# Moving the operand tiles of a two-layer hybrid decoder kernel to other SBUF addresses with small spacer tiles

## The chip, the cores and the metric

One Trainium2 chip, one core of it. The metric is the device time of one execution in microseconds (us); smaller is better.

## What is computed

Two layers (DEPTH = 2) of a decoder trunk on a residual stream of 256 tokens by 2048 channels, all float32. In each layer the stream is normalised and modulated to `u`, and one wide projection `u @ w_in` feeds three token mixers. Cut to what matters here:

```python
u = rms_norm(x, norm_w) * (1.0 + scale) + shift          # scale, shift, gate from silu(c) @ w_ada
proj = u @ w_in                                           # w_in: 2048 x 19,064
y_fox = fox_attention(fq, fk, fv, log_f) * silu(fg)
y_dsa = dsa_attention(dq, dk, dv, iq, ik, iw) * silu(dg)  # keys chosen by an indexer
y_ssd = rms_norm(ssd_scan(conv(sxbc), dt, a, b, c) * silu(sz))
merged = (sigmoid(mg0) * (y_fox @ w_o_fox) + sigmoid(mg1) * (y_dsa @ w_o_dsa)
          + sigmoid(mg2) * (y_ssd @ w_o_ssd))
return x + gate * (merged @ w_out)
```

## The kernel before

All weights stream once from HBM as half-pieces of 128 partitions x 1024 float32 (512 KB, line L162, tile `raw`, 7 buffers). A half-piece is split into a high part `wh` (ScalarE, L175, 4 buffers) and a low part `wl` (VectorE, L176, 3 buffers); the activations are kept as high and low parts too: `uh`, `ul` for the normalised input, `yh`, `yl` (two tiles each) for the gated attention outputs, `ysh`, `ysl` for the state-space output, `mh`, `ml` for the merged stream. A product is three matmuls on float32r operands: high x high, low x high, high x low.

There are two forms. In `feat` (L213 to L215) the **weights are stationary**: 128 columns of a half-piece are loaded into TensorE and 256 tokens of an activation tile move past them. In `three` (L180 to L182, called by `tok_half` and `tok_group`) the **activations are stationary**: 128 tokens of `uh` or `ul` are loaded, and 512 columns of the half-piece move.

```python
for k in range(nk):                                   # feat
    c = slice(k % 8 * P, k % 8 * P + P)
    mm(ps, lhsT=h[:, c], rhs=ah[:, k, :], ...)        # L213
    mm(ps, lhsT=h[:, c], rhs=al[:, k, :], ...)        # L214
    mm(ps, lhsT=l[:, c], rhs=ah[:, k, :], ...)        # L215
```

A layer goes through these stages. First the token-major projections of the queries, keys and values (`tok_half`; in layer 0 they run in `start` while the modulation from `w_ada` is still being summed on VectorE, L229). Then `feat` products for the gates and the convolution input, with the attention and state-space mixers' small products placed between them by a tick counter. Then the gated merge in three branches (`br` 0, 1, 2): for each of 16 column tiles a `feat` over `uh`, `ul` with 16 k-tiles (48 matmuls) and one over the branch's own tile (`yh`, `yl` with 8 k-tiles, 24 matmuls; `ysh`, `ysl` in branch 2 with 16 k-tiles, 48 matmuls). Last the output projection, `feat` over `mh`, `ml`, 16 times 48 matmuls. During layer 0's second half the modulation of layer 1 is streamed too, some half-pieces of `w_ada` for every weight half-piece. TensorE issues in the order written by hand; the weight stream's work on ScalarE, VectorE and the SP queue is emitted ahead of everything else, in its own order.

SBUF tiles come from pools that are laid out one behind the other from the low end (`const`, `wp` with `raw`, `wh`, `wl`, then `up` with `uh`, `ul`, then `small`, then the pools on the side "left") and from the high end (side "right", with `ysp` for `ysh`, `ysl`). A tile's address thus follows from what was allocated ahead of it. The buffers of `wh` and `wl` are 4096 bytes each per partition and all of them lie at one address modulo 1024; a k-tile of 256 tokens is 1024 bytes, a weight block of 128 columns 512 bytes.

Of the kernel before, what the change touches and what calls it, by code (L numbers as in the profile page):

```python
# [10 lines left out]
F32 = mybir.dt.float32  # L11
# [5 lines left out]
PSUM = bass.MemoryType.PSUM  # L17
DRAM = bass.MemoryType.DRAM

DM, SEQ, DEPTH, P = 2048, 256, 2, 128  # L20
# [35 lines left out]
# modulation: (layer, blocks, first tick, ticks a tile)  # L56
ADA = ((0, range(8, 12), 212, 1.8), (1, range(8), 270, 1.9), (1, range(8, 12), 600, 4.0))
# start: steps by which the modulation runs ahead of its use, loads of x after which a tile of it is loaded
AHEAD, EARLY = 1, (1,)
# ticks between dependent products of a mixer, by layer  # L60
# [9 lines left out]
class Net:  # L70
    def __init__(self, ctx, tc, xT, c, pos, inv, par, w_ada, w_tm, w_ts, w_sm, w_od, outT):
        self.tc, self.nc = tc, tc.nc
        self.xT, self.c, self.pos, self.inv, self.par = xT, c, pos, inv, par
        self.w_ada, self.w_tm, self.w_ts, self.w_sm, self.w_od, self.outT = w_ada, w_tm, w_ts, w_sm, w_od, outT
        pool = lambda **k: ctx.enter_context(tc.tile_pool(**k))
        self.const = pool(name="const", bufs=1)
        self.wp = pool(name="wp", bufs=1)
        self.up = pool(name="up", bufs=1)
        self.small = pool(name="small", bufs=1)
        self.mm = pool(name="mm", bufs=4, space=PSUM)  # L80
        self.mx = pool(name="mx", bufs=4, space=PSUM)
        self.dram = pool(name="dram", bufs=1, space=DRAM)
        self.ada_queue = []
        self.front = -1000000
        self.nticks = 0
        self.lanes = [[], [], []]
        # TensorE issues in emission order: ticks place the mixers' products between the projections'
        ctx.enter_context(tc.manual_schedule(engines={mybir.EngineType.PE}))

# [21 lines left out]
    def spawn(self, n, gen, *after):  # L111
        """queue a mixer's steps; it starts when the jobs it follows have been emitted"""
        job = Layer()
        job.gen, job.after, job.done = gen, after, False
        self.lanes[n].append(job)
        return job
# [17 lines left out]
    @contextmanager  # L134
    def first(self):
        """what the weights' stream needs goes before everything else, in its own order"""
        tc = self.tc
        outer, tc.cur_priority = tc.cur_priority, self.front
        yield
        self.front, tc.cur_priority = tc.cur_priority, outer  # L140
# [4 lines left out]
    def rsqrt(self, out, ss, scale, eps, tag):  # L145
        """out = (ss * scale + eps) ** -0.5"""
        nc = self.nc
        shape = list(ss.shape)
        x, y, t = [self.st(shape, tag + n) for n in ("_x", "_y", "_t")]
        i = t.bitcast(I32)  # L150
        nc.vector.tensor_scalar(x, ss, scale, eps, op0=OP.mult, op1=OP.add)
        nc.vector.tensor_scalar(i, x.bitcast(I32), 1, None, op0=OP.logical_shift_right)
        nc.vector.tensor_scalar(y.bitcast(I32), i, -1, 0x5F3759DF, op0=OP.mult, op1=OP.add)
        for n in range(3):
            nc.vector.tensor_mul(t, y, y)
            nc.vector.scalar_tensor_tensor(t, t, -0.5, x, op0=OP.mult, op1=OP.mult)
            nc.vector.scalar_tensor_tensor(out if n == 2 else y, t, 1.5, y, op0=OP.add, op1=OP.mult)

# [6 lines left out]
    def half(self, src):  # L165
        """half a piece, as high and low parts"""
        with self.first():
            r = self.raw(src)
            h = self.wp.tile([P, 1024], F32R, tag="wh", name="wh", bufs=NWH)
            l = self.wp.tile([P, 1024], F32R, tag="wl", name="wl", bufs=NWL)  # L170
            self.split(h, l, r)
        return h, l
# [11 lines left out]
    def tok_half(self, out, src, k, k0, k1):  # L184
        """two k tiles x 512 columns, activations stationary"""
        h, l = self.half(src)
        for i in range(2):
            c = slice(i * 512, i * 512 + 512)
            for th in range(2):
                s = slice(th * P, th * P + P)  # L190
                self.three(out[th], self.uh[:, k + i, s], self.ul[:, k + i, s], h[:, c], l[:, c], k + i == k0, k + i == k1)

    def tok_group(self, blocks):
        """out[b][th] is a bank [token, 512 columns]"""
        out = [[self.mmbank() for _ in range(2)] for _ in blocks]
        for k in range(0, KT, 2):
            for b, blk in enumerate(blocks):
                src = self.w_tm[self.l, blk, k // 2]
                self.tok_half(out[b], src, k, 0, KT - 1)
                self.tick()  # L200
        return out

    def feat(self, src, ah=None, al=None, nk=KT):
        """weights stationary: a bank half [128 columns, 256 tokens]"""
# [16 lines left out]
    def ada_raw(self, l, blk, n, r=None):  # L221
        """modulation: half of the sum for the feature tile blk * 4 + n // 2; after every second tile the pair is put together"""
# [35 lines left out]
    def load(self, x, ssq, *tmp):  # L258
        """what the first products wait for: silu of c on all partitions, x and its sum of squares"""
# [97 lines left out]
    def rstd_row(self, ssq):  # L357
        """1 / rms of each token, along the free axis of every partition"""
# [15 lines left out]
    def u_tile(self, l, k, t):  # L374
        """u = x * A * rstd + shift, as high and low parts"""
        nc = self.nc
        b = self.mods[l].mod[:, k:k + 1]
        nc.scalar.activation(self.uh[:, k, :], t, AF.Identity, bias=b)  # L378
        nc.vector.scalar_tensor_tensor(self.ul[:, k, :], t, b, self.uh.bitcast(F32)[:, k, :], op0=OP.add, op1=OP.subtract)
# [9 lines left out]
    def start(self, blocks, x, ssq, row, raws, got):  # L389
        """first layer: the modulation arrives by pairs of feature tiles; the first products over each four tiles  # L390
        run as soon as their part of u is there, and add up in SBUF (those of the first two blocks in PSUM)"""
# [64 lines left out]
    def head_rstd(self, t, nh, pool):  # L456
        """1 / rms of each head of t [token, 2, nh * 128]"""
# [11 lines left out]
    def to_heads(self, dst, h0, t, c0, scale=None):  # L469
        """two 128-column blocks of token-major t -> dst[:, h0:h0+2, tokens]"""  # L470
# [11 lines left out]
    def rope(self, v, half, c0, pool):  # L482
        """v [token, 2, heads, dims]: rotate the first 2 * half dims"""
# [32 lines left out]
    def g_small(self, ps, sm, dtt, par, lay, D, pool):  # L516
        """softplus of sdt, log sigmoid of ff, their cumulative sums"""
# [33 lines left out]
        # forget gate: cumulative sums, token-major and as rows (those of the keys)  # L551
# [7 lines left out]
        # state-space decays: cumulative sums by chunk, token-major and as rows  # L559
# [18 lines left out]
    def g_heads(self, n, logits, vals, dst, pool):  # L578
        """causal attention, a head a tick: logits, then softmax and its transpose, then the product with the values"""
# [73 lines left out]
    def g_index(self, iqT, ikT, sm, acc, pool):  # L653
        """scores of the indexer; acc becomes 0 at the selected causal keys and BIG elsewhere"""
# [50 lines left out]
    def gate_y(self, name, y, pool):  # L705
        """y *= 2 * silu(gate); y came with a factor of a half"""
# [10 lines left out]
    def layer(self, l):  # L717
# [3 lines left out]
        # right: y of the attentions, temporaries of both; left: one mixer's operands  # L721
# [27 lines left out]
        if l == 0:  # L749
            # x lies where the transposed heads come later  # L750
# [3 lines left out]
        def got(name, j=0, t=None):  # L754
            """a block of projections is there, token-major: the next steps of its mixer"""
# [5 lines left out]
            elif name == "iq":  # L761
                # indexer queries, transposed, lie where the attention's output comes later
# [47 lines left out]
        for g in range(4):  # L810
# [10 lines left out]
            if g == 0:  # L821
                ysp, close_ys = self.pool("ysp", "right")
                S.ysh = ysp.tile([P, KT, SEQ], F32R, name="ysh")
                S.ysl = ysp.tile([P, KT, SEQ], F32R, name="ysl")
            self.spawn(2, self.g_norm(l, g, S.gate, S.y, sp, S), S.job)
# [6 lines left out]
        gp, close_g = self.pool("gp", "left")  # L832
        hp, close_h = self.pool("hp", "left")
        yhl = []
# [7 lines left out]
        for br in range(3):  # L842
            if br == 2:
                close_h()
                mp, close_m = self.pool("mp", "left")
                mh = mp.tile([P, KT, SEQ], F32R, name="mh")
# [54 lines left out]
    def conv(self, f, dst, sp):  # L901
        """causal depthwise convolution over 128 channels, then SiLU"""
# [112 lines left out]
    def g_norm(self, l, g, gates, y, sp, S):  # L1015
        """gate and group norm, transposed"""
# [42 lines left out]
def _ada_raws(w):  # L1059
    """w [2048, 6144] by feature tile and half of k, transposed"""  # L1060
# [3 lines left out]
def _pack(i):  # L1064
# [12 lines left out]
    # halves [128, 1024] of pieces: two k tiles x 512 columns, or eight k tiles x 128 columns  # L1077
# [29 lines left out]
```

## Time and profile before

| | |
|---|---|
| median of 3 runs | 2466.78 us (2463.59 to 2470.31) |
| profiled execution, span from the first to the last instruction | 2465.1 us |
| TensorE busy | 2418.5 us, 98% of the span, 17256 matmuls |
| VectorE busy | 1752.3 us, 71% |
| ScalarE busy | 1195.9 us, 49% |
| mean HBM traffic | 214 GB/s |
| mean granted TensorE clock | 0.997 of full speed |

The profiled execution's own time is its span, 2465.1 us; the median of the runs shown lies 1.7 us above it. A matmul's busy time runs from its start to its modelled end, and consecutive matmuls overlap: durations of 283 ns stand beside starts that are some 120 ns apart. So what a matmul costs is read from the spacing of the starts, which is the length of a stretch over the number of matmuls in it (a count of a window holds about two that began before it).

### The profile page before, as it was taken

How to read it: one execution, taken by the hardware profiler on the slowest of the kernel's cores; microseconds unless marked ns; L12 is line 12 of the kernel's file. 1: busy time of each engine (PE TensorE's matmuls, PEld its weight loads, DVE VectorE, ACT ScalarE, POOL GpSimd, SP SyncE). 2: the span in 40 equal slices, each digit the busy share in tenths (PEclk: the TensorE clock that was granted, in tenths of full speed). 3: DMA queues.
4: the chain of work that ended last, by engine and by line, in shares of the span. 5: the costliest groups of instructions: out<-in, count | busy, mean ns of one | idle time of the engine just before them, and what ended most of it. 6: DMA issues, size and time to landing. Idle time of an engine off the chain costs nothing.

```text
span 2465.1 us, 43733 instructions
## 1 busy us (share of the span) xinstructions
PE 2418.5 (98%) x17256; PEld 2247.5 (91%) x17256; DVE 1752.3 (71%) x3109; ACT 1195.9 (49%) x1932; POOL 1.8 (0%) x11
## 2 busy tenths in 40 slices
PE   6999999999999999999989999999999999999999
PEld 4778799998899999999978877999999999999999
DVE  8899978777766777776775567767776655666554
ACT  4535656555544444343344655555555444444443
POOL 0000000000000000000000000000000000000000
PEclk9999999999999999999999999999999999999999
DMA  9998434544468888788865544544544667776564
GB/s 341 331 328 290 146 120 138 161 157 159 157 214 281 289 281 288 271 276 269 306 205 184 188 138 146 177 152 153 161 155 162 227 229 238 231 233 229 187 214 155
DMA packets 145216, 527.79 MB, mean 214 GB/s; under 512 B 16369, under 2 KB 16881, under 8 KB 145009
## 3 DMA queue, kind: packets, MB, share of 16 engines
q1 hardware_dynamic: 145010, 525.00, 63.4%
q8 instruction: 135, 2.21, 0.4%
q14 instruction: 71, 0.58, 0.1%
HBM read 520.74 MB, written 4.19 MB: 213 GB/s over the span
## 4 chain that ended last, share of the span: by engine, by line
PE 89%; DVE 5%; DMA 4%; issue 1%; ACT 0%; SPq 0%; DVEq 0%
PE pm L213 19%; PE pm L215 19%; PE pm L214 19%; PE pm L180 8%; PE pm L182 8%; PE pm L181 8%; DMA raw<-w_ada 3%; DVE wl L176 2%; DVE raw L229 2%; PE px L987 1%; PE px L475 1%; PE px L609 1%; PE px L996 1%; DMA raw<-w_od 1%; PE held L181 0%
## 5 line engine op out<-in xcount | busy, mean ns | idle before, releaser
L175 ACT CAST wh<-raw 128x1024 fp32r<-128x1024 f32 x788 | 825.4, 1050 | 1002.0 <-PE pm L214 547.5
L176 DVE TENSOR_TENSOR wl<-raw,wh 128x1024 fp32r<-128x1024 f32 x788 | 959.9, 1222 | 344.1 <-PE pm L215 152.9
L213 PE MATMUL pm<-uh,wh 128*128 128x256 f32 x2848 | 816.5, 287 | 0.0
L215 PE MATMUL pm<-uh,wl 128*128 128x256 f32 x2848 | 805.7, 283 | 1.1 <-DVE wl L176 1.1
L214 PE MATMUL pm<-ul,wh 128*128 128x256 f32 x2848 | 805.0, 283 | 0.0
L213 PEld LDWEIGHTS pm<-uh,wh 128*128 128x128 f32 x2848 | 545.1, 191 | 5.2 <-issue 3.9
L214 PEld LDWEIGHTS pm<-ul,wh 128*128 128x128 f32 x2848 | 545.3, 191 | 2.1 <-issue 1.9
L215 PEld LDWEIGHTS pm<-uh,wl 128*128 128x128 f32 x2848 | 545.1, 191 | 1.6 <-DVE wl L176 1.5
L180 PE MATMUL pm<-wh,uh 128*128 128x512 f32 x896 | 361.1, 403 | 1.1 <-ACT uh L378 1.1
L182 PE MATMUL pm<-wl,uh 128*128 128x512 f32 x896 | 352.1, 393 | 6.9 <-DVE wl L176 6.8
L229 DVE SCALAR_TENSOR_TENSOR raw<-raw,crep 128x1024 f32<-128x1024 f32 x192 | 234.0, 1223 | 174.8 <-DMA raw<-w_ada 174.8
L181 PE MATMUL pm<-wh,ul 128*128 128x512 f32 x896 | 350.7, 391 | 0.0
L182 PEld LDWEIGHTS pm<-wl,uh 128*128 128x128 f32 x896 | 169.0, 189 | 46.2 <-DVE wl L176 10.2
L180 PEld LDWEIGHTS pm<-wh,uh 128*128 128x128 f32 x896 | 169.1, 189 | 39.9 <-issue 3.0
L181 PEld LDWEIGHTS pm<-wh,ul 128*128 128x128 f32 x896 | 169.3, 189 | 35.3 <-issue 1.9
L215 PE MATMUL pm<-mh,wl 128*128 128x256 f32 x512 | 142.5, 278 | 5.2 <-DVE wl L176 4.9
L215 PE MATMUL pm<-ysh,wl 128*128 128x256 f32 x512 | 144.7, 283 | 1.2 <-DVE wl L176 1.2
L214 PE MATMUL pm<-ysl,wh 128*128 128x256 f32 x512 | 144.2, 282 | 0.0
L213 PE MATMUL pm<-ysh,wh 128*128 128x256 f32 x512 | 144.1, 281 | 0.0
L214 PE MATMUL pm<-ml,wh 128*128 128x256 f32 x512 | 141.6, 277 | 1.4 <-DVE ml L176 1.4
L213 PE MATMUL pm<-yh,wh 128*128 128x256 f32 x512 | 142.0, 277 | 0.0
L214 PE MATMUL pm<-yl,wh 128*128 128x256 f32 x512 | 141.8, 277 | 0.0
(315 smaller groups left out, 2814.9 us busy)
## 6 DMA issues: line engine op xcount, KB each, us to landing
raw<-w_ts SPq DMA_DIRECT2D x352, 512.0 KB, 3.9
raw<-w_tm SPq DMA_DIRECT2D x240, 512.0 KB, 3.6
raw<-w_ada SPq DMA_DIRECT2D x192, 512.0 KB, 4.6
raw<-w_od SPq DMA_DIRECT2D x192, 512.0 KB, 4.5
raw<-w_sm SPq DMA_DIRECT2D x4, 512.0 KB, 4.7
xr<-xT SPq DMA_DIRECT2D x4, 512.0 KB, 7.0
x<-xn SPq DMA_DIRECT2D x4, 512.0 KB, 6.4
xr<-x SPq DMA_DIRECT2D x4, 512.0 KB, 6.1
```

What stands on the lines that cost most here:

```text
L175: self.nc.scalar.copy(h, src)
L176: self.nc.vector.tensor_sub(l, src, h.bitcast(F32))
L180: mm(ps, lhsT=ah, rhs=bh, start=start, stop=False)
L181: mm(ps, lhsT=al, rhs=bh, start=False, stop=False)
L182: mm(ps, lhsT=ah, rhs=bl, start=False, stop=stop)
L213: mm(ps, lhsT=h[:, c], rhs=ah[:, k, :], start=k == 0, stop=False)
L214: mm(ps, lhsT=h[:, c], rhs=al[:, k, :], start=False, stop=False)
L215: mm(ps, lhsT=l[:, c], rhs=ah[:, k, :], start=False, stop=k == nk - 1)
L229: nc.vector.scalar_tensor_tensor(r, r, 0.5, self.crep[:, n % 2 * 1024:n % 2 * 1024 + 1024], op0=OP.mult, op1=OP.mult, accum_out=m.part[:, ...
L475: nc.tensor.transpose(ps[:, j * SEQ + th * P:j * SEQ + th * P + P], t[:, th, c0 + j * P:c0 + j * P + P], self.ident)
L609: nc.tensor.matmul(po[:, :SEQ], lhsT=v[:, 0], rhs=pT[:, :SEQ], start=True, stop=False)
L987: nc.tensor.matmul(pd[:, c * 256 + o % 256:c * 256 + o % 256 + 64], lhsT=dec[:, i, c, :], rhs=xd[:, c, o:o + 64], start=True, stop=True)
```

## The change

Five calls of a new helper `pad` put an unused tile into a pool, cleared once by GpSimd so that it exists. Nothing is computed from it; its only effect is on the addresses of the tiles behind it (of `ysh`, `ysl` ahead of it, since that pool grows from the high end). Three of the calls stand in `layer` and run once per layer, so that there are eight clears in all. The rest of the full diff removes comments, and so shifts line numbers by a few.

```diff
         self.const = pool(name="const", bufs=1)
+        self.pad(self.const, 32)
         self.wp = pool(name="wp", bufs=1)
         self.up = pool(name="up", bufs=1)
+        self.pad(self.up, 192)
...
+    def pad(self, pool, nbytes):
+
+        t = pool.tile([P, nbytes // 4], F32, name="pad")
+        self.nc.gpsimd.memset(t, 0.0)
+
...
                 S.ysl = ysp.tile([P, KT, SEQ], F32R, name="ysl")
+                self.pad(ysp, 928)
...
         hp, close_h = self.pool("hp", "left")
+        self.pad(hp, 832)
...
                 mp, close_m = self.pool("mp", "left")
+                self.pad(mp, 832)
```

The start addresses of the tiles in the two built programs, in bytes of a partition modulo 1024, and the distance from the weights to the moving operand:

| tile | before | after | distance before | distance after |
|---|---|---|---|---|
| `wh`, `wl` (and `raw`) | 736 | 768 | | |
| `uh`, `ul` in `feat` | 736 | 960 | 0 | 192 |
| `yh`, `yl` | 928 | 960 | 192 | 192 |
| `ysh`, `ysl` | 864 | 960 | 128 | 192 |
| `mh`, `ml` | 928 | 960 | 192 | 192 |
| `wh`, `wl` moving past `uh`, `ul` (`three`) | 736 | 768 | 0 | -192 |

Without the modulo, the tiles began before at byte 65248 (`wh`), 81632 (`wl`), 93920 (`uh`, which with `ul` ends at 126688), 137120 (`yh`, `mh`) and 174944 (`ysh`). A distance is that of the tiles' starts; the weight blocks and token halves inside the tiles step by 512 bytes, so each distance comes with itself plus 512.

The instructions of TensorE, ScalarE and the SP queue stand in the same order in both programs, and on VectorE one pair of set-up instructions is swapped. GpSimd has the new clears. Its queue in the changed program, from the identity matrix on (`logf` is the clear for the log-forget sums of a layer, the rows `pad 128x232` and `pad 128x208 x2` are those of `ysp` and of `hp` and `mp`):

```order
6 masks.py:197 MEMSET ident 128x128
7 L128 MEMSET pad 128x8
8 L128 MEMSET pad 128x48
9 L551 MEMSET logf 128x80
10 masks.py:199 ISA
11 masks.py:199 AFFINE_SELECT ident<-ident 128x128
12 L306 AFFINE_SELECT tri<-tri 128x128
13 L311 AFFINE_SELECT msk<-msk 128x128 x2
14 L128 MEMSET pad 128x232
15 L128 MEMSET pad 128x208 x2
16 L551 MEMSET logf 128x80
17 L128 MEMSET pad 128x232
```

Before, rows 7, 8, 14, 15 and 17 are not there (nor a last one like row 15, which follows row 17), and nothing else differs in this queue.

## Rows read from the trace of the kernel before

**Rows 1.** The page: the engines' busy time, and the chain that ended last

```profile
PE 2418.5 (98%) x17256; PEld 2247.5 (91%) x17256; DVE 1752.3 (71%) x3109; ACT 1195.9 (49%) x1932; POOL 1.8 (0%) x11
...
PE 89%; DVE 5%; DMA 4%; issue 1%; ACT 0%; SPq 0%; DVEq 0%
```

**Rows 2.** Busy time by stretch: start, layer 0's merge and output projection, layer 1's merge

```profile
core 0: us, PE busy (x) PEld busy (x) DVE busy (x) ACT busy (x) POOL busy (x), PEclk, DMA share, GB/s
0.00:230.00 230.00, 201.83 (x832) 160.06 (x833) 207.09 (x360) 103.13 (x145) 1.61 (x10) 0.99 0.92 332
700.00:1026.00 326.00, 326.00 (x2761) 325.78 (x2760) 233.01 (x333) 139.32 (x162) 0.00 (x0) 1.00 0.82 277
1026.00:1250.00 224.00, 215.12 (x1799) 211.76 (x1798) 162.91 (x257) 88.83 (x112) 0.00 (x0) 1.00 0.84 284
1905.00:2180.00 275.00, 275.00 (x2335) 275.00 (x2334) 170.74 (x218) 119.20 (x138) 0.00 (x0) 1.00 0.70 230
```

**Rows 3.** Matmuls by moving or stationary tile: duration ns min/median/max (views of uh, yh, ysh, mh)

```profile
L213 PE MATMUL pm<-uh,wh x2848: 277/283/682, 230.0 to 2368.7; 128*128 128x256 f32 x190
L213 PE MATMUL pm<-yh,wh x512: 276/276/286, 705.1 to 2191.2; 128*128 128x256 f32 x171
L213 PE MATMUL pm<-ysh,wh x512: 274/281/287, 976.8 to 2374.4; 128*128 128x256 f32 x171
L213 PE MATMUL pm<-mh,wh x512: 276/276/337, 1158.4 to 2461.5; 128*128 128x256 f32 x171
L180 PE MATMUL pm<-wh,uh x896: 387/389/803, 39.2 to 1867.0; 128*128 128x512 f32 x180
```

**Rows 4.** Stretches of one kind alone: uh/ul moving, mh/ml moving, weights moving past uh/ul

```profile
1882.00:1904.00 22.00, 22.00 (x185) 22.00 (x185) 16.19 (x34) 9.81 (x16) 0.00 (x0) 1.00 0.51 169
2400.00:2460.00 60.00, 60.00 (x532) 60.00 (x531) 29.70 (x32) 20.49 (x20) 0.00 (x0) 1.00 0.53 173
1322.00:1342.00 20.00, 20.00 (x90) 16.56 (x89) 15.12 (x49) 7.88 (x9) 0.00 (x0) 1.00 0.59 196
```

**Rows 5.** The chain in layer 0's merge, branch 0: start us, us, what

```profile
705.21 0.12 PE pm L213
713.69 0.12 PE pm L213
722.17 0.12 PE pm L213
```

**Rows 6.** The timeline in layer 1's merge: a matmul and the next one's weight load

```profile
2150.22 0.28 PE L213 MATMUL pm<-uh,wh 128*128 128x256 f32 x1
2150.22 0.19 PEld L214 LDWEIGHTS pm<-ul,wh 128*128 128x128 f32 x1
2150.34 0.28 PE L214 MATMUL pm<-ul,wh 128*128 128x256 f32 x1
```

**Rows 7.** Costliest groups of the two forms: busy us, mean ns

```profile
L214 PE MATMUL pm<-ul,wh 128*128 128x256 f32 x2848 | 805.0, 283 | 0.0
L214 PE MATMUL pm<-ysl,wh 128*128 128x256 f32 x512 | 144.2, 282 | 0.0
```

**Rows 8.** Waits from 700 to 1026: who waited for whom, us in total, times, longest

```profile
ACT wh L175 <- PE pm L214: 120.4, 67, 1.9
DVE raw L229 <- DMA raw<-w_ada: 81.8, 55, 4.2
```

**Rows 9.** The chain from 1026 to 1255: shares by line

```profile
by line: DMA raw<-w_ada 35.4%; PE pm L215 11.1%; PE pm L213 10.2%; PE pm L214 10.2%; issue 9.6%; DVE wl L176 7.6%; DMA raw<-w_od 5.5%; DMA xr<-xT 4.5%; DVE raw L229 3.3%; DVE mt L861 0.5%; DVE ml L176 0.5%; SPq L162 0.3%; ACT wh L175 0.3%; 
```

**Rows 10.** GpSimd's clear of logf: busy us, mean ns, idle before it

```profile
L544 POOL MEMSET logf<- 128x80 f32 x2 | 0.3, 166 | 264.3 <-PE px L558 264.3
```

## The prediction

> **What bounds the kernel now.** I read the shares first: TensorE is busy 98% of the span and makes up 89% of the chain that ended last, VectorE and DMA 9% together [rows 1]. Then the stretches: in the first 230 us VectorE is busy 207 us and DMA 92%, so the start is not TensorE's; from 700 to 1026, and in layer 1's merge, TensorE never stops; from 1026 to 1250 it is idle 9 us [rows 2]. So a nanosecond taken off each matmul reaches the end nearly everywhere but in the start and in that last stretch.
>
> The next question is what a matmul costs. Stretches of one kind give the spacing of starts. With `mh`, `ml` moving, 60.00 us hold 530 matmuls once the two that began earlier are taken off: 113.2 ns. With `uh`, `ul` moving, 22.00 us hold 183: 120.2 ns. With 512 weight columns moving past `uh`, `ul`, 20.00 us hold 88: 227 ns [rows 4]. The granted clock is 1.00 of the upper level, 2.4 GHz, in all three, so 256 columns alone take 106.7 ns and 512 take 213.3. What stands above that is 6.5, 13.5 and 14 ns. The reader should see that the excess is not tied to the length of the matmul: it doubles between two streams of the same shape and is the same for 256 and for 512 columns.
>
> What differs between the streams of the same shape? Not the neighbours: in the merge, products over `uh` and over `yh` alternate every few us beside the same work on other engines, and medians are 283 and 276 ns; `mh` gives 276, and `ysh` lies between with 281 [rows 3]. Three starts 8.48 us apart hold 48 matmuls over `uh`, `ul` and 24 over `yh`, `yl` each [rows 5]; with 113.2 ns for the 24 the other 48 come to 120.1. In the table of addresses the order is the same: distance 0 costs 283, 128 costs 281, 192 costs 276, twice. And the timeline shows what can meet: the weight load of the next matmul starts with the current matmul, at 2150.22 both [rows 6], so two reads of SBUF run side by side, from places that the distance sets. My reading is that the excess is their conflict, 13.4 ns when both begin at the same residue, half of that 192 bytes apart.
>
> The Trainium skill speaks against that. The page SBUF — State Buffer, section "Who interferes with whom", gives TensorE two independent read ports, one for the moving operand and one for weights, and calls the port pair of VectorE and GpSimd the only contention there is. By it no distance could matter, the terms below would all be zero, and the time would stay at 2467; the medians of 276 and 283 side by side disagree with it.
>
> **The change part by part.**
>
> *`uh`, `ul` in `feat`: distance 0 to 192.* There are 3 lines x 2848 = 8544 matmuls [rows 3]. Priced as the `mh` stream they lose 283 - 276 = 7 ns by duration, or 120.1 - 113.2 = 6.9 by spacing, at most 59 us. But the shortest now take 277, and those behind a mixer's insertion run shorter than the steady 120 already; I take 6.3 ns: **-54 us**.
>
> *`ysh`, `ysl`: 128 to 192.* 3 x 512 = 1536 matmuls, mean 282 [rows 7] against 276 for `mh` at 192. The minimum of 274 says that they vary; I take 5.2 ns: **-8 us**.
>
> *`yh`, `yl`, `mh`, `ml`: 192 stays.* Their absolute address moves by 32 bytes. The few matmuls by which `yh` today settles in behind a `uh` product vanish: 64 products, some 20 ns each: **-1 us**.
>
> *The 512-column form: 0 to -192.* 30 blocks of 96 matmuls make 2880, of which the 10 blocks of layer 0's start (960) are covered by VectorE and DMA; 1920 count. No stream here has the moving operand behind the weights. The ends: all of the 14 ns goes (-26 us), or it grows by another 6.7, the step between distances 192 and 0 (+13 us). The nearest rows are those 192 bytes apart the other way, which lose 6.7; with one matmul in four left out, since it stands next to a mixer's insertion, 1500 x 6.7 gives **-10 us**.
>
> *What is late next.* From 1026 to 1255 the chain is held by weight and modulation transfers: the lines on DMA hold 45% of it, TensorE's 32% [rows 9], so what TensorE saves there comes back as waiting for `wl`. That stretch has about 70% of branch 2's 768 matmuls over `uh` and 768 over `ysh`: 540 x 6.3 + 540 x 5.2 ns = 6 us given back. Before it, from 700 to 1026, ScalarE waits 120 us for TensorE to free `wh`, so TensorE leads; but VectorE is busy 233 us and waits 82 for `w_ada`, 315 of 326 [rows 2, 8]. A TensorE faster by 5% would ask for 277 x 1.05 = 291 GB/s where the start got 332; I take back a third of the 11 us that this stretch's 1640 or so matmuls over `uh` would gain, 4 us. Together **+10 us**. Layer 1's merge draws 230 GB/s and has room.
>
> *The clears.* Eight on GpSimd; its clear of `logf` with 80 columns takes 166 ns [rows 10], so these, of 8 to 232, cost some 0.2 us each on an engine busy 1.8 us in all. In the queue the second layer's `logf` now stands behind the pads of layer 0's `hp` and `mp`, which wait for the tiles whose place they take. Those are free by the start of layer 0's branch 2, long before layer 1's `logf` is due; it waited 264 us for its turn in the trace [rows 10]. If that cover were gone, `logf` would be late by one clear, 0.2 us. **0 us**. The start gains nothing for the same reason that it is not TensorE's.
>
> Sum: -54 - 8 - 1 - 10 + 10 = -63, and 2465.1 - 63 = 2402.1 for the profiled execution. The median of the runs lies 1.7 us above that execution's span: **2404 us**.
>
> **The rivals.**
>
> *The distance is not what matters (11%).* `uh` and the weights lie below byte 126,700 of a partition, all faster tiles above 137,000; the cost could belong to that neighbourhood, or to the tile. For it: `uh` stays where it is, but for 224 bytes. Against it: `ysh` lies highest of all and is slow. Then only `ysh` would move, 2459, or nothing, 2467: half of the chance each.
>
> *Deeper (11%).* The old starts, 736, 864 and 928, are all 32 bytes past a multiple of 64; the new ones, 768 and 960, are multiples of 64. If the 6.5 ns left at distance 192 come from starts that lie across such a boundary, all 13,152 `feat` matmuls (8544 + 3 x 1536) lose more. No stream of this form runs without the 6.5, so the ends are 0 and 6.5; two thirds of it, 4.3 ns, would be 56 us, less 10 in the stretches that transfers bound: 2404 - 46 = 2358. The minimum of 274 with `ysh` speaks weakly for it. The page TensorE: Matmul & The Clock Gate, section "Back-to-back issue gap", gives N / 2.4 + 2.5 for a matmul at full clock, an estimate of 109.2 ns here, which no stream of this form in the trace reaches.
>
> *Slower (5%).* The residue of the address itself sets the cost, and 928 is a good one. At 960 `yh` and `mh` would go the way of today's `uh`, 3072 x 6.7 ns = +21 us with `uh` left at 120, and the 512-column form pays its upper end, +13: 2467 + 34 = 2501. It decides if the medians over `yh` and `mh` rise above 280.
>
> **How the numbers follow.** The forecast's case has 73%. A measurement here can tell about 0.3% from no change, 7.4 us. Faster by more than that: 73 + 11 + half of the first rival (2459 lies just past the bound), 5.5, makes 0.89; the same 0.06; slower 0.05. The range: the forecast's case runs from 2378 (the 512-column form gains all, nothing is given back) to 2434 (that form loses 13, and the 11 us of the stretch from 700 on come back whole). This alone would leave out 27%, so the range goes down to the deeper rival's 2358 with a little room, 2354.
>
> **What would show it.** Right, if the medians over `uh`, `ysh`, `yh` and `mh` are all 276, 60 us of pure `uh` hold about 530 matmuls, and the idle time of TensorE between 700 and 1250 rises from 9 us to some 19. The 512-column form's 389 is the open term: 382 for my figure. Wrong, if `uh` stays at 283, or if `mh` leaves 276 either way.

## The result and the profile after

The changed kernel takes **2430.64 us** (median of 4 runs, 2427.7 to 2431.68) beside 2466.42 (4 runs, 2463.59 to 2470.31): ratio 0.9852, 95% interval 0.9839 to 0.9865, 35.8 us less. The profiled execution has a span of 2429.0 us.

The page of the changed kernel, the lines that answer to [rows 1]:

```profile
PE 2377.0 (98%) x17256; PEld 2201.7 (91%) x17256; DVE 1748.7 (72%) x3109; ACT 1196.6 (49%) x1932; POOL 3.5 (0%) x19
...
PE 83%; DMA 7%; DVE 7%; issue 2%; ACT 0%; SPq 0%; DVEq 0%; ACTq 0%
```

TensorE is busy 41.5 us less for the same 17256 matmuls. It leads less of the chain, 83% for 89%, and DMA more. The views of the tiles in the changed kernel, as in [rows 3] (duration in ns, min/median/max):

```profile
L220 PE MATMUL pm<-uh,wh x2848: 276/276/682, 230.7 to 2333.0; 128*128 128x256 f32 x190
L220 PE MATMUL pm<-yh,wh x512: 276/276/286, 696.6 to 2164.3; 128*128 128x256 f32 x171
L220 PE MATMUL pm<-ysh,wh x512: 276/276/415, 966.3 to 2338.4; 128*128 128x256 f32 x171
L220 PE MATMUL pm<-mh,wh x512: 276/276/419, 1148.8 to 2425.4; 128*128 128x256 f32 x171
L187 PE MATMUL pm<-wh,uh x896: 387/392/797, 38.6 to 1852.7; 128*128 128x512 f32 x180
```

All four moving tiles have the median of 276 now; the 512-column form went the wrong way, 389 to 392. Stretches of the changed kernel: pure `uh`/`ul`, pure `mh`/`ml`, weights moving (as in [rows 4]), then the three that answer to [rows 2]:

```profile
core 0: us, PE busy (x) PEld busy (x) DVE busy (x) ACT busy (x) POOL busy (x), PEclk, DMA share, GB/s
1867.00:1888.00 21.00, 21.00 (x187) 21.00 (x187) 16.27 (x33) 10.21 (x16) 0.00 (x0) 1.00 0.52 175
2364.00:2424.00 60.00, 60.00 (x532) 60.00 (x531) 29.62 (x32) 20.41 (x20) 0.00 (x0) 1.00 0.51 174
1312.00:1332.00 20.00, 20.00 (x89) 16.43 (x88) 15.25 (x49) 8.12 (x10) 0.00 (x0) 1.00 0.59 192
700.00:1026.00 326.00, 321.95 (x2764) 319.42 (x2763) 231.77 (x337) 134.15 (x156) 0.00 (x0) 1.00 0.83 281
1026.00:1250.00 224.00, 210.37 (x1774) 208.49 (x1772) 162.75 (x258) 90.88 (x114) 0.00 (x0) 0.98 0.83 283
1905.00:2180.00 275.00, 275.00 (x2429) 275.00 (x2428) 175.91 (x227) 122.77 (x140) 0.00 (x0) 1.00 0.72 243
```

With two taken off each count, `uh` runs at 21.00 / 185 = 113.5 ns where it took 120.2. The weights moving take 20.00 / 87 = 230 ns, up from 227; a window this short is good to one matmul in 87, and from the trace's start times the steady spacing is 228.9 ns, up from 226.7. Layer 1's merge holds 2429 matmuls in 275 us where it held 2335. From 700 to 1026 there are 2764 for 2761: nothing gained, and 4.05 us of idle where there was none. The waits of the changed kernel from 700 to 1150 show what TensorE met there (us in total, times, longest):

```profile
ACT wh L182 <- PE pm L221: 126.6, 73, 2.9
DVE raw L236 <- DMA raw<-w_ada: 118.2, 72, 4.7
...
PEld pm L222 <- DVE wl L183: 11.9, 15, 2.4
PE pm L222 <- DVE wl L183: 8.8, 11, 2.2
```

TensorE waits for `wl`, and VectorE, which makes `wl`, waits 118 us for `w_ada`.

The same by stage, from the trace's start times (from the first matmul of a stage to the first of the next; the nine differences make -35.8):

| stage | before | after | difference | of it |
|---|---|---|---|---|
| layer 0 start | 227.3 | 228.2 | +0.9 | 512-column form +1.0 |
| layer 0 projections, mixers | 469.3 | 460.5 | -8.7 | `uh` -9.4, 512-column form +0.6 |
| layer 0 merge, branches 0 and 1 | 271.8 | 269.4 | -2.4 | `uh` -5.3, `yh` +3.0 |
| layer 0 merge, branch 2 | 187.3 | 188.2 | +0.9 | `uh` -3.3, `ysh` +4.2 |
| layer 0 output projection | 99.5 | 100.0 | +0.5 | |
| layer 1 projections, mixers | 662.3 | 654.7 | -7.5 | `uh` -8.6, 512-column form +1.1 |
| layer 1 merge, branches 0 and 1 | 271.4 | 261.1 | -10.3 | `uh` -9.7, `yh` -0.6 |
| layer 1 merge, branch 2 | 183.2 | 174.1 | -9.2 | `uh` -5.0, `ysh` -4.2 |
| layer 1 output projection | 87.0 | 86.9 | 0.0 | |

The +0.9 of layer 0's start is no more than that stage differs between executions: it takes 227.8 to 229.9 us in the runs below. Wherever transfers do not hold TensorE, `uh` gains. In layer 0's merge nearly all of it is lost again, and that has two causes (the experiments on `w_ada`).

### The profile page after: what moved, and what is told of

Same layout as the page of the kernel before. It is cut to its first block, busy times and chain, and to the rows that moved or that the text cites. A ratio compares the mean times of both kernels' runs of the same rounds, so it can differ in the third digit from the quotient of the medians.

```text
span 2429.0 us, 43742 instructions
## 1 busy us (share of the span) xinstructions
PE 2377.0 (98%) x17256; PEld 2201.7 (91%) x17256; DVE 1748.7 (72%) x3109; ACT 1196.6 (49%) x1932; POOL 3.5 (0%) x19
## 4 chain that ended last, share of the span: by engine, by line
PE 83%; DMA 7%; DVE 7%; issue 2%; ACT 0%; SPq 0%; DVEq 0%; ACTq 0%
PE pm L222 17%; PE pm L220 17%; PE pm L221 17%; PE pm L187 8%; PE pm L189 8%; PE pm L188 8%; DMA raw<-w_ada 6%; DVE wl L183 3%; DVE raw L236 2%; PE px L997 1%; DMA raw<-w_od 1%; PE px L482 1%; PE px L616 1%; PE px L1006 1%; PE px L608 0%
## 5 line engine op out<-in xcount | busy, mean ns | idle before, releaser
L183 DVE TENSOR_TENSOR wl<-raw,wh 128x1024 fp32r<-128x1024 f32 x788 | 959.2, 1222 | 312.3 <-PE pm L189 119.0
L220 PE MATMUL pm<-uh,wh 128*128 128x256 f32 x2848 | 801.6, 281 | 0.0
L222 PE MATMUL pm<-uh,wl 128*128 128x256 f32 x2848 | 791.2, 278 | 2.0 <-DVE wl L183 1.9
L221 PE MATMUL pm<-ul,wh 128*128 128x256 f32 x2848 | 790.0, 277 | 0.0
L220 PEld LDWEIGHTS pm<-uh,wh 128*128 128x128 f32 x2848 | 535.6, 188 | 5.2 <-issue 3.9
L222 PEld LDWEIGHTS pm<-uh,wl 128*128 128x128 f32 x2848 | 535.6, 188 | 3.4 <-DVE wl L183 3.0
L221 PEld LDWEIGHTS pm<-ul,wh 128*128 128x128 f32 x2848 | 536.2, 188 | 2.1 <-issue 1.9
L222 PE MATMUL pm<-yh,wl 128*128 128x256 f32 x512 | 142.2, 278 | 1.5 <-DVE wl L183 1.4
L220 PE MATMUL pm<-mh,wh 128*128 128x256 f32 x512 | 143.0, 279 | 0.0
```

What stands on the lines that cost most here:

```text
L183: self.nc.vector.tensor_sub(l, src, h.bitcast(F32))
L220: mm(ps, lhsT=h[:, c], rhs=ah[:, k, :], start=k == 0, stop=False)
L221: mm(ps, lhsT=h[:, c], rhs=al[:, k, :], start=False, stop=False)
L222: mm(ps, lhsT=l[:, c], rhs=ah[:, k, :], start=False, stop=k == nk - 1)
```

## The experiments

All are edits of the changed kernel unless said otherwise. A spacing is the time between starts of consecutive matmuls of one stream in its steady parts, from the trace's start times.

**Without the 32 bytes.** Every start falls back to 32 bytes past a multiple of 64, with the distances kept at 192.

```diff
-        self.pad(self.const, 32)
...
-                self.pad(ysp, 928)
+                self.pad(ysp, 960)
```

> The changed kernel without the 32 bytes ahead of the weights: weights back at 736 modulo 1024, every moving tile of the weight-stationary products at 928, so all distances are 192 as in the change and only the starts lie 32 bytes past a multiple of 64 again. Theory A (the distance alone sets the spacing): medians of uh, yh, ysh and mh all 276, the 512-column form at 392 to 394 as in the change, time 2431 within 5. Rival B (the 32 bytes, that is the start's place within 64 or 256 bytes, have a part in it): the 512-column form goes back to 389 as before the change, 2880 x 2 ns = 3 to 6 us faster than the change, or the medians over uh leave 276.

2429.47 us (2423.97 to 2434.32), ratio to the kernel before 0.9858, interval 0.9839 to 0.9877: the same as the change. The four medians are 276 and the 512-column form's is 394, with a steady spacing of 228.9 ns as in the change. So it plays no part in the time whether the tiles start at 736 and 928 or at 768 and 960.

**Other distances.** The same pads with other sizes put `uh`, `yh`, `mh`, `ysh` at 256, 0, 64, 320, at 128, 256, 448, 384, and at 320, 96, 160, 224. The first of the three diffs (the other two have 128, 736, 960, 128 and 320, 896, 608, 672 in its four places):

```diff
-        self.pad(self.up, 192)
+        self.pad(self.up, 256)
...
-                self.pad(ysp, 928)
+                self.pad(ysp, 800)
...
-        self.pad(hp, 832)
+        self.pad(hp, 576)
...
-                self.pad(mp, 832)
+                self.pad(mp, 640)
```

> Other distances by spacer sizes alone: uh, ul 256 past the weights (so the 512-column form at -256), yh, yl at 0, mh, ml at 64, ysh, ysl at 320. Theory A (distance alone, modulo 512 since weight blocks step by 512): yh rises from 276 to 283 though it stays the same tile in the same place of the memory; ysh at 320 mirrors 192 and shows about 276; mh at 64 lies between 276 and 283; uh at 256 shows 276 or less. 512-column form between 387 and 392. Rival C (the tile or its region, not the distance): yh and mh stay at 276, uh stays at 276 as in the change. Time by A: mh and yh lose some 3072 x 4 to 7 ns = 12 to 21 us against the change, so 2440 to 2452; by C 2431.

> uh, ul at distance 128 (512-column form at -128), yh, yl at 256, mh, ml at 448, ysh, ysl at 384. Theory A: uh shows the 281 that ysh showed at 128 before the change, yh at 256 shows 276 or less, ysh at 384 mirrors 128 (281) and mh at 448 mirrors 64. Rival A' (only a moving operand ahead of the weights helps, not modulo 512): ysh at 384 and mh at 448 show 276 or less. Time by A 2435 to 2460, by A' 2445 or less.

> uh, ul at distance 320 (512-column form at -320, which modulo 512 is 192), yh, yl at 96, mh, ml at 160, ysh, ysl at 224. Theory A with modulo 512: the 512-column form, at 192 now, behaves as the weight-stationary one does at 192 and falls below 389, to about 382, if the same collision is at work; uh at 320 shows about 276; yh at 96 lies above mh at 160, mh above ysh at 224 (276). If the 512-column form stays at 389 to 394 at this distance too, its excess over 213 ns has another cause than the distance. Time by A about 2415 to 2430 if the 512-column form gains, 2430 to 2440 if not.

256, 0, 64, 320: 2476.52 us (2475.8 to 2476.72), ratio 1.0049, interval 1.0032 to 1.0065. The other two, one run each: 2472.0 and 2468.81, beside 2464.36 for the kernel before on the same chip. The tiles `yh` and `uh` in the first of them, then its stretches of pure `mh` (64), `uh` (256) and weights moving:

```profile
L220 PE MATMUL pm<-yh,wh x512: 283/283/283, 706.6 to 2198.2; 128*128 128x256 f32 x171
...
L220 PE MATMUL pm<-uh,wh x2848: 277/283/679, 231.7 to 2375.3; 128*128 128x256 f32 x190
```

```profile
2408.00:2468.00 60.00, 60.00 (x511) 60.00 (x511) 29.13 (x32) 19.97 (x19) 0.00 (x0) 1.00 0.51 171
1884.00:1906.00 22.00, 22.00 (x185) 22.00 (x185) 16.19 (x34) 9.75 (x16) 0.00 (x0) 1.00 0.55 169
1324.00:1344.00 20.00, 20.00 (x90) 16.54 (x89) 15.23 (x49) 7.99 (x10) 0.00 (x0) 1.00 0.62 193
```

`yh` has not changed its neighbourhood or its work, and its median rose from 276 to 283 because it now stands at distance 0. That is the case against "the tile or the region". `uh` at 256 costs what it cost at 0. In the second kernel `mh` stands at 448 = 256 + 192; its tile view and its pure stretch:

```profile
L220 PE MATMUL pm<-mh,wh x512: 276/276/415, 1158.7 to 2466.7; 128*128 128x256 f32 x171
```

```profile
2406.00:2464.00 58.00, 58.00 (x514) 58.00 (x514) 28.90 (x31) 20.05 (x19) 0.00 (x0) 1.00 0.56 177
```

58.00 / 512 = 113.3 ns: fast again. So the distance counts modulo 256. In the third kernel the 512-column form has -320, which is 192 modulo 256; its tile view and its stretch:

```profile
L187 PE MATMUL pm<-wh,uh x896: 388/398/801, 38.7 to 1867.0; 128*128 128x512 f32 x180
```

```profile
1320.00:1340.00 20.00, 20.00 (x87) 16.10 (x87) 14.90 (x49) 7.83 (x9) 0.00 (x0) 1.00 0.57 186
```

20.00 / 85 = 235 ns, again good to one matmul; from the start times it is 233.3. So here 192 is the worst of the four distances tried. All spacings, in ns, by moving minus stationary start modulo 256, from the start times:

| | 0 | 64 | 96 | 128 | 160 | 192 | 224 |
|---|---|---|---|---|---|---|---|
| `feat`, 256 columns | 120.0 | 117.7 | 119.9 | 118.8 | 117.3 | **113.3** | 118.2 |
| `three`, 512 columns | **226.7** | 228.9 | | 232.5 | | 233.3 | |

One pair of runs also parts the distance from the address. The tile `mh` starts at 928 modulo 1024 both in the run without the 32 bytes and in the third kernel here; the weights start at 736 in the first and at 768 in the second, so the distances are 192 and 160. The stretches of pure `mh` of the two, in this order:

```profile
2364.00:2422.00 58.00, 58.00 (x514) 58.00 (x513) 28.90 (x31) 20.05 (x19) 0.00 (x0) 1.00 0.55 173
```

```profile
2400.00:2460.00 60.00, 60.00 (x514) 60.00 (x513) 29.45 (x32) 20.21 (x20) 0.00 (x0) 1.00 0.52 171
```

58.00 / 512 = 113.3 and 60.00 / 512 = 117.2 ns, for the same tile at the same start.

**Beside 192.** Tiles 256 bytes wider allow starts 8 to 16 bytes off: `uh` stays at 192, `mh`, `yh`, `ysh` go to 208, 176, 200, and in a second kernel to 176, 208, 184. The helper and one use of it:

```diff
+    def shifted(self, pool, nk, name, o):
+        t = pool.tile([P, nk * SEQ + 64], F32R, name=name)
+        return t[:, o:o + nk * SEQ].rearrange("p (k t) -> p k t", t=SEQ)
...
-                mh = mp.tile([P, KT, SEQ], F32R, name="mh")
+                mh = self.shifted(mp, KT, "mh", 12)
```

> Distances between the steps of 32 that the allocator gives, by starting inside a wider tile: mh, ml at 208, yh, yl at 176, ysh, ysl at 200; uh, ul stay at 192 as in the change. So far the spacing in us per 1000 matmuls was 117.3 at 160, 113.3 at 192, 118.2 at 224. Theory N (a narrow best place at 192): mh at 208 and yh at 176 lie between, 114 to 117, medians 277 to 280, ysh at 200 at 113 to 115; time 2432 to 2442. Rival W (the best place lies beside 192, and the floor of about 109 is reached there): one of them shows a median of 272 to 274, and the layer-1 stage with it gains 3 us per 768 matmuls; time 2422 to 2431.

> The same with mh, ml at 176, yh, yl at 208, ysh, ysl at 184. Theory N: as f_208, and each distance costs the same whichever tile has it (mh at 176 as yh at 176 in f_208). Rival W: a median of 272 to 274 at one of them. Time 2432 to 2442 by N, 2422 to 2431 by W.

2444.77 and 2445.22 us, one run each, beside 2462.51 for the kernel before. The pure `mh` stretch of the first, and under it that of the second:

```profile
2376.00:2436.00 60.00, 60.00 (x505) 60.00 (x505) 28.91 (x31) 20.00 (x19) 0.00 (x0) 1.00 0.49 166
```

```profile
2376.00:2436.00 60.00, 60.00 (x506) 60.00 (x505) 28.90 (x31) 19.99 (x19) 0.00 (x0) 1.00 0.50 166
```

60.00 / 503 = 119.3 and 60.00 / 504 = 119.0 ns. No better place was found beside 192: 16 bytes away the spacing is what it is at 128, and `ysh`, 8 bytes away at 200 and at 184, takes 120.0 ns by its start times, as at 0. Of the places tried, 192 stands alone. One rival is not excluded: in these two kernels the moved tiles start 8 or 16 bytes past a multiple of 32, which no tile of these products does in the other runs, and that could cost something by itself. The neighbours 160 and 224 (117.3 and 118.2 ns) are free of this doubt.

**`uh` alone.** The spacers ahead of the constants and of `ysh` go; the other three stay.

```diff
-        self.pad(self.const, 32)
...
-                self.pad(ysp, 928)
```

> Only uh and ul are moved: the spacer ahead of the constants and the one in the pool of ysh, ysl are left out, so the weights stay at 736, uh and ul go from 736 to 928 (distance 192), yh and mh stay at distance 192, and ysh, ysl stay at 128 as before. Theory D (the distance of each stream sets that stream's spacing, the streams add up): the change without its ysh term, which was about 4 us in layer 1's branch 2 and nothing in layer 0's (transfers hold that stretch): 2430.6 + 4 = 2434.6, uh and ul at a median of 276, ysh at 281, layer 1's branch 2 at 174.1 + 4 = 178. Rival R (the two rhythms are started by interruptions, and one stream at 119 or so carries its rhythm into the next): the uh products behind each ysh product run at 118 too, as they did in layer 1's branch 2 with offsets of 208, 192 and 200; then that stretch is 181 to 183 and the median of uh there above 278, and the time 2437 to 2440.

2433.3 us (2431.12 to 2434.38), ratio 0.9878, interval 0.9862 to 0.9895. Layer 1's branch 2 takes 178.7 us, `ysh` there 91.2 as before and `uh` 87.5, 113 ns at the median. The tiles `ysh` and `uh` of this kernel:

```profile
L219 PE MATMUL pm<-ysh,wh x512: 274/281/286, 968.5 to 2342.0; 128*128 128x256 f32 x171
...
L219 PE MATMUL pm<-uh,wh x2848: 276/276/686, 232.3 to 2336.3; 128*128 128x256 f32 x190
```

The streams add up one by one, as the sum assumed: 29.4 us come with `uh`, and `ysh` brings its 4 us in layer 1. A slow `ysh` did not slow the `uh` products behind it here, though it did at offset 200, where `uh` in layer 1's branch 2 took 90.3 us.

**The `w_ada` loads.** Three runs move them and one takes them away. The schedule sets from which point on they are issued and how many half-pieces go between two weight half-pieces. First spread out earlier, on the change and on the kernel before, then spread in another way:

```diff
-ADA = ((0, range(8, 12), 212, 1.8), (1, range(8), 270, 1.9), (1, range(8, 12), 600, 4.0))
+ADA = ((0, range(8, 12), 100, 3.1), (1, range(8), 202, 2.9), (1, range(8, 12), 600, 4.0))
```

```diff
+ADA = ((0, range(8, 12), 92, 2.4), (1, range(8), 169, 3.4), (1, range(8, 12), 600, 4.0))
```

> The changed kernel with the modulation's schedule alone changed: layer 0's gate blocks from tick 100 at 3.1 ticks a tile instead of 212 at 1.8, layer 1's scale and shift blocks from tick 202 at 2.9 instead of 270 at 1.9, so that the merge of layer 0 streams 1.35 half-pieces a tick instead of 1.53. Theory S: layer 0's merge and output projection get back most of what they lost, 269 to 262, 188 to 176, 100 to 93, and the projection stage of layer 0 loses at most 5: the kernel at 2405 to 2412. Rival V: VectorE has the same work and only at other times, so no more than 5 us come back: 2425 or more.

> The kernel before with the same other schedule (layer 0's gate blocks from tick 100 at 3.1, layer 1's blocks from 202 at 2.9). Theory S: it had fewer stalls to lose, some 4 us in branch 2 and 12 in the output projection; 2450 to 2458. Against this run the addresses are then worth some 45 to 50 us in the spread schedule, against 36 in the old one. If the addresses are worth 36 in both, the schedule has nothing to do with what was given back.

> As n_spread with more of it moved ahead: layer 0's gate blocks from tick 92 at 2.4 ticks a tile, layer 1's from 169 at 3.4, so 1.29 half-pieces a tick in the merge. Theory S: the merge and output projection as in n_spread or 2 to 4 us better, the projection stage 2 to 6 us worse since VectorE is fuller there; 2403 to 2414. Rival V: 2425 or more.

The first schedule on the change: 2464.09 us (10 runs, 2459.12 to 2470.59), ratio 1.0004, interval 0.9992 to 1.0016, as slow as the kernel before. On the kernel before: 2502.91 (2498.89 to 2510.65), ratio 1.0169, interval 1.0145 to 1.0194. The second on the change: 2442.4 (2441.46 to 2444.81), ratio 0.9915, interval 0.9899 to 0.993. The expectation that an earlier, thinner stream frees the merge missed. It lengthened layer 0's projections to 472.9 and 479.4 us from 460.5; the first schedule lengthened branches 0 and 1 too, to 288.7, and the second left them at 270.1. What the pair does show is that the addresses are worth 38.8 us under that schedule, 35.8 under the old one. The 45 to 50 us expected of the pair missed too, and by that expectation's own test a difference near 36 says that this other schedule changed nothing in what was given back.

In the fourth run layer 1's scale and shift get no `w_ada` from HBM: their 64 half-pieces are not loaded, and VectorE does the same kind of operation on a tile that is there already, so layer 1 computes something other than the reference does.

```diff
-            r = r or self.raw(self.w_ada[l, blk, n])
+            bare = l == 1 and blk < 8
+            r = self.wp.tile([P, 1024], F32, tag="raw", name="raw", bufs=NRAW) if bare else r or self.raw(self.w_ada[l, blk, n])
...
-            nc.vector.scalar_tensor_tensor(r, r, 0.5, self.crep[:, n % 2 * 1024:n % 2 * 1024 + 1024], op0=OP.mult, op1=OP.mult,
+            nc.vector.scalar_tensor_tensor(r, self.crep[:, :1024] if bare else r, 0.0005 if bare else 0.5, self.crep[:, n % 2 * 1024:n % 2 * 1024 + 1024], op0=OP.mult, op1=OP.mult,
```

> The changed kernel with the 64 half-pieces of w_ada for layer 1's scale and shift left out: their sums are formed on VectorE from a resident tile instead, with a small factor, so VectorE's work and its waiting on buffers stay and only the transfers go; layer 1's scale and shift are then not those of the reference. Theory S (the gain of layer 0's merge and the output projection's stalls are lost to transfers of w_ada: weights come late, TensorE stops, and after a stop it often runs on at 118 ns a matmul instead of 113): layer 0's branches 0 and 1 fall from 269 to about 261 us, branch 2 from 188 to about 174, both as in layer 1, the output projection from 100 to about 90; the kernel to about 2397. Rival V (VectorE's own load holds these stages): they stay within 3 us of 269, 188 and 100, the kernel at 2425 to 2431.

2415.2 us (2403.3 to 2417.24), ratio 0.9791, interval 0.9755 to 0.9827: between the 2397 of the one expectation and the 2425 of its rival. Two stretches of it in layer 0's merge and one in layer 1's, and the matmuls around 853.9 us (start us, us, engine, line):

```profile
700.00:850.00 150.00, 148.87 (x1306) 148.12 (x1305) 107.17 (x152) 64.05 (x73) 0.00 (x0) 1.00 0.85 285
860.00:1012.00 152.00, 152.00 (x1293) 152.00 (x1292) 116.69 (x169) 64.25 (x75) 0.00 (x0) 1.00 0.63 200
...
1885.00:2136.00 251.00, 251.00 (x2217) 251.00 (x2216) 160.89 (x207) 111.97 (x127) 0.00 (x0) 1.00 0.75 242
```

```profile
853.65 0.28 PE L220 MATMUL pm<-yh,wh 128*128 128x256 f32 x1
853.76 0.28 PE L221 MATMUL pm<-yl,wh 128*128 128x256 f32 x1
853.88 0.29 PE L222 MATMUL pm<-yh,wl 128*128 128x256 f32 x1
854.00 0.28 PE L220 MATMUL pm<-yh,wh 128*128 128x256 f32 x1
854.12 0.28 PE L221 MATMUL pm<-yl,wh 128*128 128x256 f32 x1
854.24 0.28 PE L222 MATMUL pm<-yh,wl 128*128 128x256 f32 x1
```

From 860 on nothing stops TensorE, and yet 152.00 us hold 1291 matmuls, 117.7 ns each, where layer 1's merge has 251.00 / 2215 = 113.3 with the same tiles at the same addresses. The timeline shows the turn: starts 0.11 us apart up to 853.76, 0.12 from there on. They stay so until layer 0 ends at about 1232 us. Nothing longer than one spacing of 124 ns stands at this turn, so a delay of some 10 ns is enough for one. In the changed kernel itself the turn comes with a longer delay; this timeline shows one of 0.27 us:

```profile
897.53 0.28 PE L222 MATMUL pm<-uh,wl 128*128 128x256 f32 x1
897.64 0.28 PE L220 MATMUL pm<-yh,wh 128*128 128x256 f32 x1
897.76 0.28 PE L221 MATMUL pm<-yl,wh 128*128 128x256 f32 x1
898.03 0.38 PE L222 MATMUL pm<-yh,wl 128*128 128x256 f32 x1
898.25 0.28 PE L220 MATMUL pm<-yh,wh 128*128 128x256 f32 x1
898.37 0.28 PE L221 MATMUL pm<-yl,wh 128*128 128x256 f32 x1
898.49 0.28 PE L222 MATMUL pm<-yh,wl 128*128 128x256 f32 x1
```

So at distance 192 there are **two rhythms**, 113.3 and 117.8 ns, and each can stay for hundreds of us. In the changed kernel all but one of 49 turns stand at an interruption, a spacing of 140 ns or more or a mixer's insertion; the one left has a spacing of 124 ns. Layer 0's merge and output projection take 557.6 us with the change (269.4 + 188.2 + 100.0), 541.2 without the loads (267.3 + 180.9 + 93.0), and layer 1's take 522.1 (261.1 + 174.1 + 86.9). The loads, with VectorE's waiting for them, cost 16.4 us in these two executions (15.4 between the medians of the runs). 19.1 more are lost without them: 14 by the rhythm from 854 to 1232 (some 378 us / 117.8 ns x 4.4 ns), and, by the start times, 2 in interruptions before 854 and 3 in one wait of the next layer's first product for the sum of squares (`ssq`) at its end.

**An interruption on purpose.** Three matmuls of 128 columns, whose results are not used (the trace shows six instructions), at column tile 4 of each branch of layer 1's merge:

```diff
+                if l == 1 and c == 4:
+                    pb = self.pbank()
+                    for i in range(3):
+                        nc.tensor.matmul(pb[:, i * P:i * P + P], lhsT=self.ident, rhs=self.ident, start=True, stop=True)
```

> The changed kernel with three small matmuls of a resident tile, read by nobody, put ahead of the fifth column tile in each of the three branches of layer 1's merge, where TensorE has no stall and runs at 113.3 ns throughout: three interruptions of about 0.4 us. Theory L (TensorE keeps one of two rhythms, 113 or 118 ns a matmul, and an interruption can throw it into the other, where it stays to the next one): from at least one of the three points on, matmuls start 118 ns apart to the next interruption or the end of the stage, 3 to 20 us more than the 1.2 us of the insertions themselves, so 2434 to 2452. Rival I (an interruption costs only itself, and 118 has to do with the load in layer 0): spacing back at 113 after each, 2430 to 2433.

2424.95 us in one run, 37.6 us below the kernel before on the same chip, where the change gained 35.8. The insertions end at 1928.9, 2060.1 and 2202.3 us; the stretches behind two of them:

```profile
1929.00:2060.00 131.00, 131.00 (x1158) 131.00 (x1157) 79.24 (x99) 56.29 (x65) 0.00 (x0) 1.00 0.75 241
...
2203.00:2330.00 127.00, 127.00 (x1123) 127.00 (x1122) 72.75 (x91) 57.87 (x70) 0.00 (x0) 1.00 0.67 211
```

131.00 / 1156 and 127.00 / 1121 are both 113.3 ns. An interruption need not turn the rhythm; this expectation missed. Others turn it every time: an insertion of eight 64-column matmuls among the mixers (`px<-xd,dec`) stands in 8 pairs, its two members some 3.7 us apart. By the start times the first of a pair turned 113.3 into 117.8 ns 8 times of 8, and the second, the same eight matmuls, turned 117.8 back into 113.3 8 times of 8. It did so in this run, in the changed kernel, in the run without the 32 bytes and in the one without the loads. So what follows can depend on the rhythm before; what decides in general stays open.

## Why the prediction was right, and where it was not

The direction and the main step held: the cost hangs on the distance from the weights to the moving tile, `yh` and `mh` stayed at 276, and `uh` and `ysh` came down to it. That the cost is a conflict of two reads, as the prediction has it, was argued from the timeline, and no run shows it. The time lies inside the range, but 26.6 us above the 2404 that was named and only 3.4 below the range's upper end: the large errors below all went one way. By the steps:

- **`uh`, `ul`, -54 us.** Outside layer 0's merge 6240 of these 8544 matmuls run, and they gained 9.4 + 8.6 + 9.7 + 5.0 = 32.7 us, 5.2 ns each where 6.3 were taken (39 us). In layer 1's merge it is 9.7 us / 1536 = 6.3 ns, as taken. Among the mixers it is 18.0 us / 3936 = 4.6 ns, 6.8 us less than at 6.3. The allowance left out the slower rhythm: of 232 undisturbed pieces of 12 matmuls there 71 run in it, 71 x 12 x 4.4 ns = 3.7 us.
- **`ysh`, -8 us.** In layer 1 -4.2 us for 768, 5.5 ns each where 5.2 were taken; without the move, in the run with `uh` alone, 0.0. In layer 0 the gain drowned in the waits.
- **`yh`, -1 us.** -0.6 us in layer 1, as thought. The `yh` of layer 0 lost 3.0 to the waits.
- **The 512-column form, -10 us: the step that failed.** It assumed that a distance of -192 would do what 192 does, since no stream of that kind stood in the trace. It cost +2.7 us (1.0 + 0.6 + 1.1 over all 2880; the 1.0 of the start is within what that stage varies). The other distances show what held in its place: this form is best at 0, where it was, and slower at 64, 128 and 192 modulo 256 (226.7, 228.9, 232.5, 233.3 ns), and -192 is 64 modulo 256. The nearest row was one of another form, and the sign did not carry over.
- **What comes back in layer 0's merge, +10 us: too small.** Gross, 2304 x 6.3 ns of `uh` and 768 x 5.2 of `ysh` make 18.5 us. The stages gained 2.4 - 0.9 = 1.5, so 17.0 came back. Waits are the part that was foreseen: TensorE's idle time from 700 to 1250 rose from 9 to 4.05 + 13.63 = 17.7 us, against "some 19"; from the merge's first matmul to the end of the output projection, which the window cuts off in the kernel before, it rose from 11.3 to 17.1. By the start times, spacings of 140 ns and more take some 11 us more in the merge than before, about the 10 of the forecast. The other part, some 7 us, was not foreseen: the slower rhythm, behind such delays as that at 897.8. A delay costs its own length and then can cost 4.4 ns on every matmul until the rhythm turns back. The run without loads shows the rhythm without the waits. (The stretch from 700 to 1026 has 1770 matmuls over `uh`, not the 1640 that the forecast wrote; its 11 us go with 1770.)
- **The clears, 0 us.** GpSimd is busy 3.5 us, and no wait in the merge names it.

The missing 27 us are thus: `uh` outside layer 0's merge 39.3 - 32.7 = 6.6, the 512-column form 12.7, layer 0's merge 7.0. That makes 26.3; the slower rhythm is in the first and the last of the three.

Of the rivals, "the distance is not what matters" fell with `yh` at distance 0, "deeper" with the run without the 32 bytes, where the 6.5 ns above 106.7 stayed whole, and "slower" with `mh`, which starts at 960 now and kept 276, and with its two spacings at one start. The Trainium skill, page SBUF — State Buffer, section "Who interferes with whom", by whose two independent read ports no distance could matter, disagrees with 113.3 ns at 192 and 120.0 at 0, and with 2476.52 us for other pads of the same kind.

What stays open: why 192 and why modulo 256, whether two reads collide at all, what decides between the two rhythms, and why the 512-column form prefers 0. No version tried that computes the same beats the change by more than its runs scatter.

## What to carry to other kernels

Where identical matmuls have medians that differ by tile, look at the start addresses of the two operands before looking at the neighbours, and try a spacer: here 6.7 ns of 120 went for a few hundred bytes. Measure the place instead of sliding towards it, for each form of matmul by itself: the best distance stood alone, with 32 bytes off already slow, and a place that is good for one form was bad for the other. What is saved ahead of a stretch that transfers hold is not saved.

## What was not expected of the hardware

- The spacing follows the distance modulo 256 bytes (120.0 ns at 0 and 256, 113.3 at 192 and 448), with a narrow low: 117.3 at 160, 118.2 at 224, and 119.0 at 176 and 119.3 at 208 where the starts are off a multiple of 32 as well.
- The 512-column form has a dependence of its own, lowest at 0: 226.7, 228.9, 232.5, 233.3 ns at 0, 64, 128, 192.
- One stream at one address has two steady rhythms, 113.3 and 117.8 ns, at a granted clock of 1.00, the 2.4 GHz level, in both. In the changed kernel 194 of 968 undisturbed pieces of 12 `feat` matmuls run in the slower one: 194 x 12 x 4.4 ns = 10 us. Behind an insertion of ten small matmuls that follows a block of the 512-column form it was the fast one 8 times of 8 in the changed kernel and the slow one 6 times of 8 in the kernel without the 32 bytes.
- Both rhythms are there at distance 64 too, where the slower one is the rule: in the kernel with `uh` at 320, 26 of 421 undisturbed pieces of 12 over `uh` run at 113.3 ns and the rest at 117.8, which is the 117.7 of the table. What differs between 64 and 192 is how often each rhythm is met.
- The Trainium skill, page TensorE: Matmul & The Clock Gate, section "Back-to-back issue gap", gives N / 2.4 + 2.5 for the gap of a matmul by itself, an estimate of 109.2 ns for 256 columns, and says that with weight loads in the stream both operations set the spacing. The best of all runs here, with a weight load ahead of each matmul, is 113.3.
